# Single-row FFN gate sums, a reordered opening, and a final norm in four multiplications in a two-layer backbone kernel

## The chip, the cores and the metric

The kernel runs on one core of a Trainium2 chip, as one program. The metric is device time of one execution in microseconds (us), the median of the runs shown; lower is better. On a core, TensorE (PE) multiplies matrices, VectorE (DVE), ScalarE (ACT) and GpSimd (POOL) work on elements, and SyncE (SP) issues the DMA transfers here. Each engine executes its own instructions in order and waits on semaphores for the others.

## The reference

Two layers over 640 tokens (128 context, 512 latent) of width 1024. Each layer has a mixer (layer 0: pooling and short convolution; layer 1: grouped-query attention) and a SwiGLU FFN, each behind an RMSNorm with a shift, a scale and a gate that come from a conditioning vector; one last RMSNorm ends it.

```python
def ada_params(cvec, w_ada, b_ada):
    m = jax.nn.silu(cvec) @ w_ada + b_ada
    return jnp.split(m[:, None, :], 6, axis=-1)

for l in range(DEPTH):
    sh1, sc1, g1, sh2, sc2, g2 = ada_params(cond, w_ada[l], b_ada[l])
    h = rms_norm(x, norm_g[l, 0]) * (1 + sc1) + sh1
    x = x + g1 * mixer(h)
    h = rms_norm(x, norm_g[l, 1]) * (1 + sc2) + sh2
    x = x + g2 * ((silu(a) * b) @ w_out)      # a, b = split(h @ w_in)
y = rms_norm(x, final_g)
```

Context tokens take a learned condition, latent tokens a given one, so every adaLN parameter is a pair of values. Outputs are the two parts of y and the new keys and values.

## The kernel before, in words

**Layout.** The residual stream lies in the on-chip memory as `x[128, 8, 640]`: eight blocks of 128 features, tokens along the row. All float32 products are split: an operand is kept as a high and a low half (`ah`/`al`, `wh`/`wl`), and a product is three matmul passes (high by high, low by high, high by low). One output block of 128 features by 640 tokens from 1024 input features takes 8 x 3 x 2 matmuls of 128x320.

**Weights.** `Weights` streams them from memory in order (`raw_...`, issued by SP), three raw buffers ahead; ACT rounds the high half (`wh`, L144) and DVE subtracts for the low half (`wl`, L145). PE, the only user, takes them in the order of the program.

**Stages of layer 0.** The opening computes two of the six adaLN chunks (2 is the first half of the mixer's scale, 3 the second) on PE (`ada_pe` L298, `ada_row` L322, `ada_turn` L327), scales x with them (`prep` L478: ACT writes `ah`, DVE writes `al`), multiplies the first three blocks of the mixer's input weights (`first_mm` L795) and sums the squares of x for the norm (`Norm.add` L430: the first four blocks square and add on POOL, the last four square on ACT and add on POOL). Then `project("pi")` does 13 more input blocks beside the pooling and convolution (`mixer_in` L999), and `project("po")` the eight output blocks. The FFN has three groups of 8, 8 and 6 hidden blocks: the first group begins with 4 plain blocks (8 products), all other hidden blocks are "fast" ones (`fast_blocks` L619): a unit of seven quarter-size products (numbered 1 to 7) instead of eight, each of 12 matmuls in the trace, with weight sums made on DVE (lines L236 to L242) and products combined by DVE into `uv` (L652). After each group `project("fo0_...")` multiplies eight output blocks, and `residual`/`update` (L515, L501) adds each block, times the gate, to x: three DVE instructions (L506). A PSUM tile holds an output block until it has been evacuated, so PE must wait for a late DVE or ACT when it comes round to the tile. In layer 1 the mixer is attention; its FFN is the same, with a last projection `last1` (L1432) that ends in the final norm.

**Rows of adaLN.** All other adaLN values are sums on DVE: `AdaDve.run(n)` (L357) does n rows. One row is 128 of the 6 x 1024 values of a layer, from one transfer of 512 KB (`rawa`, L354): four reductions of 128x512 over `rawa` times `silb` (L371, each with a small read of its accumulator). A list of jobs `(layer, first row, number of rows)` sets their order; when a job's last row is summed, `ada_done` (L389) makes the values usable, and a set `known` holds what may be used. At the end of a row the next transfer is issued.

**Where rows are run.** The call sites set how many rows are summed beside each block: the opening, the callback `each` of `project("pi")` (`1 + (i < 7) - (i >= 11)` for block i, 18 rows), the plain blocks of the FFN (3 rows), the fast units (the callback `fast_each`, at product 6 of a unit: every unit of group 0, every second unit of groups 1 and 2), and `project("fo0_...")` (`1 + i % 2`, 12 rows in each). In layer 1, `gates` runs the eight rows of the FFN's gate in group 0, two rows in each of its four units. `EARLY = 30` is the number of rows loaded before layer 0's FFN.

**Final norm.** `last1` treats tokens in two spans (384 and 256). `nrm.finish` makes `rstd` of a span with a matmul, three ACT and three DVE instructions; `out(cols, step)` (L1443) then multiplies block by block (two of three blocks on DVE, one on POOL, L1446) and issues an output transfer for every two blocks (L1449).

## Time and profile before

| | before |
|---|---|
| runs (3): median, lowest, highest | 1377.84 us, 1377.27, 1378.74 |
| the profiled execution: time / span | 1376.99 us / 1375.2 us |
| mean granted TensorE clock | 0.986 |
| PE busy / DVE busy | 1327.7 us (97%) / 1081.2 us (79%) |
| ACT busy / POOL busy | 636.3 us (46%) / 70.3 us (5%) |
| moved by DMA | 155.54 MB, mean 113 GB/s |
| the chain that ended last, by engine | PE 77%, DVE 16%, ACT 3%, issue 2%, DMA 1% |

The span reaches from the first to the last instruction that the profiler records; the execution's own time is 1.8 us longer. The granted clock is a share of TensorE's 2.4 GHz: 1.0 and 0.5 (1.2 GHz) are its two levels. A busy PE does useful work at either level, so a stretch can be full and still be slow. The clock and the idle time of PE are thus read together: where PE waits, and what PE gets done per microsecond in a stage against a like stage elsewhere.

### The profile page before, as it was taken

The page shows a single profiled execution, that of the slowest core. Times are in us where ns is not written, and L with a number is a line of the kernel's source. Part 1 is how long each engine was busy: PE and PEld are TensorE (multiplying, and loading weights), DVE is VectorE, ACT ScalarE, POOL GpSimd, SP SyncE. Part 2 cuts the span into 40 slices and gives each one's busy share as a digit, 9 for nine tenths or more (in the row PEclk, how much of TensorE's full clock was granted, in tenths as well). Part 3 has the DMA queues.
Part 4 walks back from the last instruction along what each step waited for, and adds up shares of the span by engine and source line. Part 5 has one row for each costly group of instructions (what it writes and reads, how often), then busy time and mean ns, then how long its engine had stood idle before and what let it go on. Part 6 is the DMA issues. An engine that isn't in the chain of part 4 may idle for free.

```text
span 1375.2 us, 22538 instructions
## 1 busy us (share of the span) xinstructions
PE 1327.7 (97%) x8929; PEld 1294.1 (94%) x8929; DVE 1081.2 (79%) x2182; ACT 636.3 (46%) x1155; POOL 70.3 (5%) x73
## 2 busy tenths in 40 slices
PE   6989999989999999999999999999999999999995
PEld 3889999989999999999998899999999999999995
DVE  4899988999988898789976777689993577446745
ACT  3532335744135531454565675477551255314543
POOL 3200000000000000000013121000000000000013
PEclk7999999999999999999999999999999999999998
DMA  9635523134533254324531110031242122311212
GB/s 363 250 117 176 195 93 123 64 106 169 172 123 114 95 187 154 108 92 140 188 95 55 43 49 34 32 134 53 106 154 77 62 76 78 123 62 62 77 47 77
DMA packets 36872, 155.54 MB, mean 113 GB/s; under 512 B 4000, under 2 KB 11168, under 8 KB 26016
## 3 DMA queue, kind: packets, MB, share of 16 engines
q1 hardware_dynamic: 36768, 154.12, 32.2%
q8 instruction: 70, 1.15, 0.3%
q14 instruction: 34, 0.28, 0.1%
HBM read 148.60 MB, written 2.88 MB: 110 GB/s over the span
## 4 chain that ended last, share of the span: by engine, by line
PE 77%; DVE 16%; ACT 3%; issue 2%; DMA 1%; SPq 0%; POOL 0%; DVEq 0%; ACTq 0%; POOLq 0%
PE fi L630 24%; PE fo L289 21%; PE fi L289 7%; PE pq L289 5%; PE pi L289 5%; DVE junk L371 5%; PE po L289 4%; DVE wl_fi_p L145 3%; PE wb L289 2%; PE wa L289 2%; PE o L1326 2%; PE s L1276 1%; PE t L1309 1%; ACT wh_fi_p L144 1%; DMA raw_ada<-wada 1%
## 5 line engine op out<-in xcount | busy, mean ns | idle before, releaser
L144 ACT ACTIVATE wh_fi_p<-raw_fi 128x512 fp32r<-128x512 f32 x252 | 153.9, 626 | 219.5 <-PE fi L630 108.6
L371 DVE CUSTOM_DVE_ANT_0 junk<-rawa,silb 128x512 f32<-128x512 f32 x336 | 237.0, 705 | 6.5 <-DMA rawa<-wada 2.2
L145 DVE TENSOR_TENSOR wl_fi_p<-raw_fi,wh_fi_p 128x512 fp32r<-128x512 f32 x252 | 170.1, 686 | 64.1 <-ACT wh_fi_p L144 63.9
L506 DVE SCALAR_TENSOR_TENSOR x<-fo,mod,x 128x128 f32<-128x128 f32 (+1 forms) x144 | 55.5, 433 | 94.1 <-PE fo L289 90.8
L144 ACT ACTIVATE wh_fo<-raw_fo 128x1024 fp32r<-128x1024 f32 (+1 forms) x48 | 47.5, 990 | 145.4 <-PE fo L289 121.2
L630 PE MATMUL fi<-bh,wh_fi_p 128*128 128x320 f32 x288 | 89.0, 309 | 0.7 <-DVE x L506 0.5
L630 PE MATMUL fi<-bh,wl_fi_p 128*128 128x320 f32 x288 | 88.9, 309 | 0.6 <-DVE wl_fi_p L145 0.6
L630 PE MATMUL fi<-ah,wl_fi_p 128*128 128x320 f32 x288 | 88.8, 308 | 0.0
L630 PE MATMUL fi<-al,wh_fi_p 128*128 128x320 f32 x288 | 88.7, 308 | 0.0
L630 PE MATMUL fi<-ah,wh_fi_p 128*128 128x320 f32 x288 | 88.4, 307 | 0.0
L630 PE MATMUL fi<-bl,wh_fi_p 128*128 128x320 f32 x288 | 88.4, 307 | 0.0
L289 PE MATMUL fo<-al,wh_fo 128*128 128x320 f32 x352 | 80.8, 310 | 0.0
L289 PE MATMUL fo<-ah,wh_fo 128*128 128x320 f32 x352 | 80.6, 310 | 0.1
L289 PE MATMUL fo<-ah,wl_fo 128*128 128x320 f32 x352 | 80.4, 309 | 0.0
L289 PE MATMUL fo<-bh,wh_fo 128*128 128x320 f32 x328 | 75.2, 310 | 0.0
L289 PE MATMUL fo<-bh,wl_fo 128*128 128x320 f32 x328 | 75.0, 310 | 0.0
L289 PE MATMUL fo<-bl,wh_fo 128*128 128x320 f32 x328 | 74.9, 310 | 0.0
L630 PE MATMUL fi<-x0h,wh_fi_p 128*128 128x320 f32 x216 | 69.0, 323 | 5.0 <-DVE uv L652 3.6
L630 PE MATMUL fi<-xh,wh_fi_p 128*128 128x320 f32 x216 | 68.0, 320 | 2.6 <-DVE uv L652 2.1
L630 PE MATMUL fi<-x0l,wh_fi_p 128*128 128x320 f32 x216 | 66.9, 311 | 0.0
L630 PE MATMUL fi<-x0h,wl_fi_p 128*128 128x320 f32 x216 | 66.9, 311 | 0.0
L289 PE MATMUL pi<-ah,wh_in 128*128 128x320 f32 (+1 forms) x256 | 62.3, 326 | 4.7 <-ACT ev L526 3.8
(375 smaller groups left out, 3808.7 us busy)
## 6 DMA issues: line engine op xcount, KB each, us to landing
raw_fi<-wfi SPq DMA_DIRECT2D x44, 1024.0 KB, 4.8
rawa<-wada SPq DMA_DIRECT2D x84, 512.0 KB, 3.4
raw_fo<-wfo SPq DMA_DIRECT2D x16, 1024.0 KB, 4.9
raw_ada<-wada SPq DMA_DIRECT2D x12, 512.0 KB, 9.9
raw_in<-win SPq DMA_DIRECT2D x6, 1024.0 KB, 6.4
raw_fo<-wfo SPq DMA_DIRECT2D x8, 768.0 KB, 4.2
raw_qkv<-wqkv SPq DMA_DIRECT2D x6, 1024.0 KB, 5.0
raw_out<-wout SPq DMA_DIRECT2D x4, 1024.0 KB, 4.8
```

Of the source, the lines that this page charges most:

```text
L144: S.activation(h, src, AF.Copy)
L145: eng.tensor_tensor(out=l, in0=src, in1=h.bitcast(F32), op=ALU.subtract)
L289: PE.matmul(ps[:, h, 0 : hi - lo], w[a][:, k, cols], rhs[b][:, k0 + k, lo:hi], start=k == 0 and a == b, stop=k == kn - 1 and a == 1,)
L371: op = V.tensor_tensor_reduce(out=self.junk, in0=raw[:, cols], in1=self.silb[:, c, cols], scale=1.0, scalar=0.0, op0=ALU.mult, op1=ALU.add ...
L506: V.scalar_tensor_tensor(out=xs, in0=got[:, 0 : b - a], scalar=mod[l][:, gate0 + m, c : c + 1], in1=xs, op0=ALU.mult, op1=ALU.add,)
L630: PE.matmul(out, w[a][:, k, :], ops.get(OPERAND[p], b)[:, k, :], start=fresh and k == 0 and a == b, stop=k == ops.kn - 1 and a == 1, skip_ ...
L1276: PE.matmul(self.ps[:, hf, 0:HT], bufB[a][:, self.h, q0 : q0 + P], kt[b][:, self.kv, hf * HT : hf * HT + HT], start=n == 0, stop=n == 2,)
L1309: PE.transpose(flat(pt)[:, s * P : s * P + P], self.pe[:, s * P : s * P + P], ident)
L1326: PE.matmul(po[:, 0 : 2 * P], vt[a][:, self.kv, s * P : s * P + P], got[b][:, s, :], start=s == 0 and n == 0, stop=s == 4 and n == 2,)
```

## The change

- **Opening.** The weights of the first input blocks are loaded ahead of the four quarters of chunk 3. PE gets matmuls of zeros into a tile that is not yet used (`turn_over`: 6, 3 and 14 of 128x512). The matmuls of chunk 3 come behind the first half of the first block instead of ahead of it. The squares of x are all made by ACT (`nrm.square`), and their sums are DVE instructions (`add_square(V)`); POOL has none. The two rows that were summed together at the end of the opening's first part have four of these sums between them.
- **Rows in layer 0.** The FFN's gate (rows 40 to 47) becomes eight jobs of one row, which are summed in `fo0_0`, each ahead of the block that needs it. `EARLY` goes from 30 to 28. Rows by stage, before and after: `pi` 18 and 16 (two rows beside blocks 5 to 7 instead of 0 to 6, none left out at the end), plain blocks of the FFN 3 and 0, fast group 0 4 and 0, `fo0_0` 12 and 12, fast group 1 4 and 8, `fo0_1` 12 and 14 (1, 1, then 2 beside each block), fast group 2 3 and 6.
- **Rows in layer 1.** The FFN's gate becomes eight jobs of one row, one beside each block of `fo1_0`, with two transfers issued ahead; group 0 has none.
- **Final norm.** `out(ks, cols)` multiplies four blocks at once on DVE by `rstd` repeated along the block axis, and issues one transfer for them: four multiplications and four transfers in place of 16 and 8. The first follows the first span's `rstd`, the other three stand behind the second span's, whose `finish` has priority.

```diff
@@ -34,7 +34,7 @@
-EARLY = 30
+EARLY = 28
@@ -500,7 +500,7 @@
-        assert (l, gate0 // 8, 8) in known
+        assert any((l, gate0 // 8, n) in known for n in range(m + 1, 9))
@@ -731,13 +731,20 @@
-                project(f"fi{l}_{gi}", xin, KB, 2 * plain, in_done, ext=True, each=each and (lambda i: each(i, True)))
+                project(f"fi{l}_{gi}", xin, KB, 2 * plain, in_done, ext=True, each=each and (lambda i: each(i, gi, True)))
...
-                project(f"fo{l}_{gi}", hid, f1 - f0, KB, lambda k, ps: residual(ps, k, l, 40), each=each)
+                project(
+                    f"fo{l}_{gi}",
+                    hid,
+                    f1 - f0,
+                    KB,
+                    lambda k, ps: residual(ps, k, l, 40),
+                    each=each and (lambda i: each(i, gi)),
+                )
@@ -759,15 +766,18 @@
-            [(0, 4, 4)] + [(0, 8 * p, 8) for p in (2, 4, 3, 5)] + [(1, 8 * p, 8) for p in (1, 0, 2, 4, 3)]
+            [(0, 4, 4)]
+            + [(0, 8 * p, 8) for p in (2, 4, 3)]
+            + [(0, 40 + b, 1) for b in range(8)]
+            + [(1, 8 * p, 8) for p in (1, 0, 2, 4, 3)]
...
+        ws.load(1, cut=True)
...
-        ws.load(1, cut=True)
@@ -795,33 +805,50 @@
+        idle = first[2][:, 0, :]
+
+        def turn_over(n):
+
+            for _ in range(n):
+                PE.matmul(idle, zeror, zeror2, start=True, stop=True)
+
+        turn_over(6)
...
-        ada_pe(3, acc[3], range(1))
+        turn_over(3)
...
-        ada_pe(3, acc[3], range(1, 4))
+        turn_over(14)
...
-            nrm.add(k, pool_only=True)
-        prep(0, bufA, 0, 0)
-        prep(1, bufA, 0, 0)
-        prep(2, bufA, 0, 0)
-        ws.split(0, ahead=False)
+            prep(k, bufA, 0, 0)
+            if k == 1:
+                ws.split(0, ahead=False)
+        ws.split(1, ahead=False)
+        for k in range(4):
+            nrm.square(k)
+        first_mm(0, range(4))
+        ada_pe(3, acc[3], range(4))
...
-        prep(3, bufA, 0, 0)
-        ws.split(1, ahead=False)
-        first_mm(0, range(0, 2))
+        nrm.add_square(V)
+        nrm.add_square(V)
+        nrm.add_square(V)
+        nrm.add_square(V)
+        first_mm(1, range(2))
...
-        first_mm(0, range(2, 4))
-        first_mm(1, range(4))
+        first_mm(1, range(2, 4))
...
-            nrm.add(k)
+            nrm.square(k)
...
-        ada.run(2, hold=False)
+        ada.run(1, hold=False)
+        nrm.add_square(V)
+        nrm.add_square(V)
+        nrm.add_square(V)
+        nrm.add_square(V)
+        ada.run(1, hold=False)
@@ -1021,7 +1048,7 @@
-            each=lambda i: ada.run(1 + (i < 7) - (i >= 11)),
+            each=lambda i: ada.run(1 + (5 <= i < 8)),
@@ -1051,8 +1078,8 @@
-                each=lambda i, plain=False: ada.run(int(i >= 5) if plain else 1 + i % 2),
-                fast_each=lambda gi, n, p: ada.run(int(p == 6 and (gi == 0 or n % 2))),
+                each=lambda i, gi, plain=False: ada.run(0 if plain else 1 + (i % 2 if gi == 0 else int(i > 1))),
+                fast_each=lambda gi, n, p: ada.run(int(p == 6 and gi > 0)),
@@ -1440,13 +1467,13 @@
-        def out(cols, step):
-            for k in range(KB):
-                xs = x[:, k, cols]
-                (G if k % 3 == 1 else V).tensor_tensor(out=xs, in0=xs, in1=rstd[:, cols], op=ALU.mult)
-                if k % step == step - 1:
-                    ks = slice(k + 1 - step, k + 1)
-                    nc.sync.dma_start(yT[:, ks, cols], x[:, ks, cols])
+        def out(ks, cols):
+            n = cols.stop - cols.start
+            xs = x[:, ks, cols]
+            V.tensor_tensor(
+                out=xs, in0=xs, in1=rstd[:, None, cols].broadcast_to((P, ks.stop - ks.start, n)), op=ALU.mult
+            )
+            nc.sync.dma_start(yT[:, ks, cols], xs)
@@ -1468,26 +1495,31 @@
-            nrm.finish((lo, hi), None)
+            with tc.high_priority():
+                nrm.finish((lo, hi), None)
...
-        for h, (lo, hi) in enumerate(spans):
-            out(slice(lo, hi), 2)
+            if not h:
+                out(slice(0, 4), cols)
+        for h, ks in ((0, slice(4, 8)), (1, slice(0, 4)), (1, slice(4, 8))):
+            out(ks, slice(*spans[h]))
...
-    gates = AdaDve([(1, 40, 8)], 76)
+    gates = AdaDve([(1, 40 + b, 1) for b in range(8)], 76)
...
+    gates.load()
+    gates.load()
...
-        fast_each=lambda gi, n, p: gates.run(int(gi == 0 and p in (1, 6))),
+        each=lambda i, gi, plain=False: gates.run(0 if plain or gi else 1),
...
```

Three places show what moves. First PE in the opening, from the first matmuls on; `adap` and `adat` are the two steps of an adaLN chunk, `pi_152` and `pi_153` the first two input blocks, `pi_154` the third's tile. Before:

```order
L306 MATMUL adap_155<-raw_ada_2_101,silc 2x512 x2
L306 MATMUL adap_155<-raw_ada_3_103,silc 2x512 x2
L306 MATMUL adap_157<-raw_ada_0_107,silc 2x512 x2
L330 MATMUL adat_171<-kc,row_167 128x2 x4
L306 MATMUL adap_157<-raw_ada_1_109,silc 2x512 x2
L306 MATMUL adap_157<-raw_ada_2_111,silc 2x512 x2
L306 MATMUL adap_157<-raw_ada_3_113,silc 2x512 x2
L289 MATMUL pi_152<-ah,wh_in_0_204 128x320 x2
L289 MATMUL pi_152<-al,wh_in_0_204 128x320 x2
```

After:

```order
L306 MATMUL adap_161<-raw_ada_2_101,silc 2x512 x2
L306 MATMUL adap_161<-raw_ada_3_103,silc 2x512 x2
L813 MATMUL pi_154<-zeror 128x512 x3
L330 MATMUL adat_178<-kc,row_173 128x2 x4
L813 MATMUL pi_154<-zeror 128x512 x14
L289 MATMUL pi_152<-ah,wh_in_0_207 128x320 x2
L289 MATMUL pi_152<-al,wh_in_0_207 128x320 x2
...
L289 MATMUL pi_152<-ah,wl_in_0_208 128x320 x2
L306 MATMUL adap_163<-raw_ada_0_110,silc 2x512 x2
L306 MATMUL adap_163<-raw_ada_1_112,silc 2x512 x2
```

The four quarters of chunk 3 (`adap_157` before, `adap_163` after) move from ahead of the turning step of chunk 2 and of the first block to behind the block's first 24 matmuls.

Second DVE in `pi`, up to the multiplication that empties the next PSUM tile (`ev`, L521, the same line in both); a `junk` row and the `got` row behind it are one reduction. Before:

```order
L914 TENSOR_TENSOR s_4_588<-s_4_588,kc 128x2x8 x2
L371 ISA junk,got_16_591<-rawa_371,silb 128x512
L371 ISA got_16_591 128x1
L915 SCALAR_TENSOR_TENSOR pl_747<-s_4_588,up_578 128x128
L371 ISA junk,got_16_591<-rawa_371,silb 128x512
L371 ISA got_16_591 128x1
L915 SCALAR_TENSOR_TENSOR pl_747<-s_4_588,up_578 128x512
L371 ISA junk,got_16_591<-rawa_371,silb 128x512
L371 ISA got_16_591 128x1
L521 TENSOR_TENSOR ev_754<-pi_676,rstd 128x640
```

After:

```order
L941 TENSOR_TENSOR s_4_613<-s_4_613,kc 128x2x8 x2
L371 ISA junk,got_16_616<-rawa_396,silb 128x512
L371 ISA got_16_616 128x1
L942 SCALAR_TENSOR_TENSOR pl_760<-s_4_613,up_603 128x128
L942 SCALAR_TENSOR_TENSOR pl_760<-s_4_613,up_603 128x512
L521 TENSOR_TENSOR ev_767<-pi_695,rstd 128x640
```

From the pooling's step on `s_4` to `ev` there are three reductions before and one after; between this `ev` and the one ahead of it there are nine and six.

Third DVE at the end of `fo0_1`: the update of its last block (`fo_1_7`), behind which the first weights of fast group 2 stand (`wl_fi_16_p`). Before:

```order
L506 SCALAR_TENSOR_TENSOR x<-fo_1_7_5294,mod_77,x 128x128
L371 ISA junk,got_32_5162<-rawa_5241,silb 128x512
L371 ISA got_32_5162 128x1
L506 SCALAR_TENSOR_TENSOR x<-fo_1_7_5294,mod_77,x 128x192
L371 ISA junk,got_32_5162<-rawa_5241,silb 128x512
L371 ISA got_32_5162 128x1
L506 SCALAR_TENSOR_TENSOR x<-fo_1_7_5294,mod_77,x 128x320
L145 TENSOR_TENSOR wl_fi_16_p_5400<-raw_fi_16_4964,wh_fi_16_p_5399 128x512
L145 TENSOR_TENSOR wl_fi_16_p_5400<-raw_fi_17_5096,wh_fi_16_p_5399 128x512
```

After:

```order
L506 SCALAR_TENSOR_TENSOR x<-fo_1_7_5321,mod_77,x 128x128
L371 ISA junk,got_32_5330<-rawa_5260,silb 128x512
L371 ISA got_32_5330 128x1
L506 SCALAR_TENSOR_TENSOR x<-fo_1_7_5321,mod_77,x 128x192
L371 ISA junk,got_32_5330<-rawa_5268,silb 128x512
L371 ISA got_32_5330 128x1
L506 SCALAR_TENSOR_TENSOR x<-fo_1_7_5321,mod_77,x 128x320
L371 ISA junk,got_32_5330<-rawa_5268,silb 128x512
L371 ISA got_32_5330 128x1
L145 TENSOR_TENSOR wl_fi_16_p_5428<-raw_fi_16_4971,wh_fi_16_p_5427 128x512
L371 ISA junk,got_32_5330<-rawa_5268,silb 128x512
```

The reductions now run on past the update: one stands between its last instruction and the weights, where there was none, and more stand among the weights.

## Rows read from the trace of the kernel before

**Rows 1.** The page, busy time, share of the span and instructions of each engine.

```profile
PE 1327.7 (97%) x8929; PEld 1294.1 (94%) x8929; DVE 1081.2 (79%) x2182; ACT 636.3 (46%) x1155; POOL 70.3 (5%) x73
```

**Rows 2.** The waits of PE: waiting operation, what it waited for, total us, times, longest.

```profile
PE fi L630 <- DVE uv L652: 5.8, 3, 3.6
...
PE pi L289 <- ACT ev L526: 3.8, 1, 3.8
...
PE ms_a L464 <- DVE ssq_a L474: 1.5, 1, 1.5
```

**Rows 3.** Timeline, opening, PE: start, duration, engine, line, operation, [idle before <- releaser].

```profile
14.43 1.03 PE L306 MATMUL adap<-raw_ada,silc 128*2 128x512 f32 x4 [3.80 <-DMA raw_ada<-wada]
15.38 1.45 PE L330 MATMUL adat<-kc,row 98*128 98x2 f32 x8
```

**Rows 4.** The same, opening, ACT.

```profile
30.57 3.73 ACT L483 ACTIVATE ah<-x,sc 128x128 fp32r<-128x128 f32 x8 [7.02 <-DVE sc L401]
...
36.02 2.61 ACT L438 ACTIVATE sq_a<-x 128x640 f32<-128x640 f32 x4
```

**Rows 5.** The same, opening, DVE and POOL.

```profile
36.88 0.69 DVE L371 CUSTOM_DVE_ANT_0 junk<-rawa,silb 128x512 f32<-128x512 f32 x1
...
37.61 1.94 DVE L371 CUSTOM_DVE_ANT_0 junk<-rawa,silb 128x512 f32<-128x512 f32 x1
...
54.06 0.17 DVE L392 TENSOR_TENSOR mod<-got,sm 128x8 f32<-128x8 f32 x1
54.14 0.48 DVE L474 SCALAR_TENSOR_TENSOR ssq_a<-ms_a,ssq_a 128x320 f32<-128x320 f32 x1
...
36.89 8.03 POOL L440 TENSOR_TENSOR ssq_a<-ssq_a,sq_a 128x640 f32<-128x640 f32 x4 [13.42 <-ACT sq_a L438]
```

**Rows 6.** The same, input projection, DVE and PE.

```profile
87.55 0.81 DVE L521 TENSOR_TENSOR ev<-pi,rstd 128x640 f32<-128x640 f32 x1
...
88.69 0.90 PE L289 MATMUL pi<-ah,wh_in 128*128 128x320 f32 x2 [3.76 <-ACT ev L526]
```

**Rows 7.** Stretches: us, busy (x instructions) of PE, PEld, DVE, ACT, POOL, clock, DMA share, GB/s.

```profile
16.00:33.00 17.00, 12.64 (x47) 9.01 (x48) 12.83 (x18) 8.63 (x17) 7.15 (x5) 0.50 1.05 389
...
87.60:94.40 6.80, 5.71 (x21) 5.72 (x22) 6.80 (x20) 0.80 (x3) 0.00 (x0) 0.50 0.35 111
...
280.70:337.50 56.80, 52.33 (x339) 50.54 (x338) 53.50 (x108) 27.05 (x53) 0.00 (x0) 0.97 0.38 132
337.50:393.90 56.40, 56.40 (x385) 56.40 (x384) 52.34 (x130) 9.52 (x12) 0.00 (x0) 1.00 0.49 168
393.90:495.30 101.40, 101.17 (x678) 98.71 (x677) 85.34 (x157) 51.37 (x102) 0.00 (x0) 1.00 0.34 115
495.30:552.60 57.30, 57.21 (x386) 56.94 (x386) 52.31 (x131) 9.77 (x12) 0.00 (x0) 1.00 0.49 166
...
974.20:1027.30 53.10, 50.62 (x340) 49.21 (x339) 53.00 (x119) 26.63 (x52) 0.00 (x0) 1.00 0.38 127
1027.30:1084.00 56.70, 56.70 (x386) 56.70 (x385) 23.14 (x41) 9.73 (x12) 0.00 (x0) 1.00 0.24 87
1084.00:1184.60 100.60, 100.51 (x676) 98.15 (x675) 73.08 (x114) 52.19 (x102) 0.00 (x0) 1.00 0.25 85
```

**Rows 8.** A stretch inside fast group 0 of layer 0, with a row of reductions.

```profile
315.00:328.00 13.00, 13.00 (x89) 12.74 (x89) 12.48 (x29) 6.80 (x14) 0.00 (x0) 1.00 0.36 121
```

**Rows 9.** Timeline, start of fast group 2 of layer 0, PE.

```profile
555.02 0.39 PE L630 MATMUL fi<-bh,wh_fi_p 128*128 128x320 f32 x1 [0.48 <-DVE x L506]
...
557.95 0.41 PE L630 MATMUL fi<-x0h,wh_fi_p 128*128 128x320 f32 x1 [0.95 <-ACT fi L642]
```

**Rows 10.** Timeline, the end: DVE and SP.

```profile
1362.17 4.83 DVE L1446 TENSOR_TENSOR x<-x,rstd 128x384 f32<-128x384 f32 x5
...
1363.61 8.53 SPq L1449 DMA_DIRECT2D yT<-x  x8
...
1368.15 3.35 DVE L1446 TENSOR_TENSOR x<-x,rstd 128x256 f32<-128x256 f32 x5
```

## The prediction

> **What bounds the kernel now.** I read the page first: PE is busy 97% of the span [rows 1], so a gain is either PE idle time that goes or PE time at the half clock that goes. The waits of PE name the idle time: behind DVE's `uv`, behind `ev`, which empties a PSUM tile, behind the norm's sum [rows 2], and in the opening behind the transfer of chunk 3 [rows 3]. Then I read the stretches [rows 7]. The reader is to see two things there. First the clock: 0.50 from 16.0 to 33.0 and from 87.6 to 94.4, and 0.97 in layer 0's fast group 0. Each of the last two comes right behind a stop of PE of 3.6 to 3.8 us [rows 2, 6]; the stop of 1.5 us at the norm [rows 2] fell in a stretch that stayed at full clock. Second, like stages at unlike speed. A fast group of 8 units (56 products) takes 100.6 us in layer 1, where DVE has no reductions and is busy 73.1 of it: 1.80 us a product. Layer 0's group 0 (28 products) takes 56.8 us, 2.03 each; layer 1's group 0 takes 53.1 us, with DVE busy 53.0 of it. So in both groups 0 DVE is the bound, and elsewhere PE is.
>
> The sum is made against the profiled execution, 1376.99 us (span 1375.2); the median of the runs is 1377.84, 0.85 us above it. A difference under 0.2%, 2.8 us, can hardly be told from no change.
>
> **The price of a row.** Group 1 of layer 0 has four rows and DVE busy 85.3 us; layer 1's has none and 73.1 [rows 7]. So a row is (85.3 - 73.1) / 4 = 3.06 us of DVE, a little over four reductions of 0.69 [rows 5].
>
> **1. Opening: +6.0 us (from -2.4 to +7).** What sets its end is a chain: chunk 3 turned, scale, ACT's `ah` of blocks 4 to 7 at 30.57 [rows 4], squares, rows of reductions, weights of block 2, the norm's sum at 54.14 [rows 5], and behind it everything. Two links get shorter.
>
> The start: `adat` of chunk 2 issues at 15.38 only because chunk 3's first quarter, in front of it on PE, waits 3.80 us for its transfer [rows 3]. That goes, so the first block can begin earlier. Chunk 3 now lands behind two weight transfers of 512 KB: 1 MB at the 389 GB/s of that stretch [rows 7] is 2.7 us later. Its first quarter landed at about 14.4, and at that rate the other three 4.0 us after; with the 2.7 all is there at about 21. The first block's first 24 matmuls run ahead of it on PE: 24 x 0.147 (56.7 us for 386 [rows 7]) are 3.5 us. With `ah`, `al` and weights by about 18 to 20 and PE at full clock, they end by about 23 and chunk 3, a quarter of which takes 1.0 us [rows 3], by about 24.5; turned and scaled it lets ACT begin at 26.1, not 30.57. So the `ah` of blocks 4 to 7 comes 4.5 us earlier.
>
> The sums: POOL's four additions of 128x640 take 8.03 us, and while they run a reduction takes 1.94 us on DVE instead of 0.69; four of them do so [rows 5], 5.0 us in excess. By the Trainium skill, "SBUF — State Buffer" (section on the engine and DMA ports), DVE with two inputs and GpSimd hold a shared port pair in turn and the loser blocks for a whole instruction; by that a reduction could be held for up to a whole POOL addition, 2.0 us, and the excess would be 8.0. The row has 1.25 each, and the row decides. These sums now cost DVE four additions at the price of a 128x640 operation, 0.81 at most [rows 6]: 3.2 us (the four of blocks 0 to 3 fall into DVE's waits for chunk 3). Net 1.8. ACT's extra squares, 4 x 0.65 [rows 4], fall into its idle 7.02 us [rows 4]. Together 4.5 + 1.8 = 6.3, less a little for the order: 6.0. The low bound is rival B below. The turning-over matmuls stand ahead of nothing that is ready: 14 of 128x512, each 1.6 times one of 128x320, are 3.3 us at full clock and 6.6 at half, while weights and `al` of the first block take until about 18.
>
> **2. Input projection: +4.7 us (+1.5 to +7).** PE stops 3.76 us because the tile that it needs is emptied by `ev`, which DVE starts at 87.55 behind nine reductions since the `ev` ahead of it [rows 6]; six are left. Three less are 3 x 0.69 less some overlap, 1.85 us: the stop becomes 1.9 us. From 88.69 to 94.4 PE then worked at half clock [rows 6, 7], which costs 5.7 / 2 = 2.85 us. I take it that a stop of 1.9 us leaves the clock alone, as the one of 1.5 us did: 1.85 + 2.85 = 4.7. If the clock falls all the same, +1.85. What is late next is the next block's `ev`, with one reduction more per block than that; DVE is full up to 166, but PE has only short waits there.
>
> **3. Fast group 0 of layer 0: +5.8 us (+4 to +6.5).** 56.8 us against 28 x 1.80 = 50.3: 6.5 lost, 3.6 of it in one wait behind `uv` [rows 2], and some 1.7 at the half clock behind that wait. Three rows of the plain blocks and four of the group, 21 us of DVE, go. The group becomes like layer 1's group 1; I leave 0.7 for its first unit, where operands are still made.
>
> **4. Fast groups 1 and 2 of layer 0: 0 (0 to -7).** They get four and three rows more. Group 1: 85.3 + 4 x 3.06 = 97.6 of 101.4 us, 96% busy, so DVE still fits. The nearest row for such a load is a unit in group 0: DVE busy 12.48 of 13.0 us with a row of reductions, PE busy all 13.0 [rows 8]. I take 0, as the cover there was enough; if it is gone, a row costs up to 3.06 each.
>
> **5. Start of fast group 2: -2.6 us (0 to -5.5).** Two rows more in `fo0_1`, eight reductions of 0.69: 5.5 us of DVE in a stage that leaves it 57.3 - 52.3 = 5.0 idle [rows 7], all in the late blocks. The last update is already late: the group's first products wait 0.48 us for x and 0.95 us for ACT [rows 9]. I put the last update half of the 5.5 later, rounded. `fo0_0` has as many rows as before, and the 14 small operations that the gate's single rows add, 0.17 us each [rows 5], are 2.4 us of the 56.4 - 52.3 = 4.1 that DVE has idle there [rows 7]: 0.
>
> **6. Fast group 0 of layer 1: +2.3 us (+1.5 to +2.8).** 53.1 against 50.3; its eight rows are what fills DVE. `fo1_0`, where they go, has DVE busy 23.1 of 56.7 [rows 7]; with 24.5 more it is 47.6, and no row here bounds PE: 0.
>
> **7. End: +2.1 us (+1 to +3.2).** Five multiplications of 384 take DVE 4.83 us beside POOL's, then five of 256 take 3.35; the eight transfers are issued from 1363.61 on for 8.53 us [rows 10]. Two multiplications of 4 x 384 at the price of 640 in 0.81 [rows 6] are 2 x 1.94 at most, two of 4 x 256 are 2 x 1.30. DVE's work after `rstd` is then 6.5 us in place of 8.2, and POOL no longer stands beside it. With only the last transfers bigger, some 1.7 to 2.5 us arrive at the end.
>
> **Sum.** 6.0 + 4.7 + 5.8 + 0 - 2.6 + 2.3 + 2.1 = 18.3. 1376.99 - 18.3 = 1358.7; against the median 1377.84 - 18.3 = **1359.5 us**.
>
> **Rivals.**
> A. DVE becomes the bound in groups 1 and 2. Evidence for it: at 96% little slack is left for the order within a unit, and in layer 1's group 0 a fully busy DVE cost 2.8 us. Against: [rows 8]. If a third of the seven rows lands on PE, 7 us: 1366.5. Chance 0.14.
> B. The clock stays at half through the opening. For: it was 0.50 from 16 to 33 with PE busy 12.6 of 17.0 us [rows 7]. Then the first block's 24 matmuls take 7.0 us and end at about 26, chunk 3 is turned about 4 us later, ACT begins where it does now, and only the sums' 1.8 us or less is won; with the turning-over matmuls, 6.6 us, in the way of ready work as well, the opening loses 2.4. Against: PE now has work where it had stopped. By the Trainium skill, "TensorE: Matmul & The Clock Gate" (Part 1, the HAM clock gate), half clock is the default and sustained activity releases it, which speaks for the turning over; the same rule lets the clock drop where PE waits 2.6 us for its first weights and again for chunk 3. With +1 in place of +6.0: 1364.5. Chance 0.14.
> C. The stop in the input projection still brings half clock: 1359.5 + 2.85 = 1362.4. Chance 0.08.
> D. Slower. The nine rows more in group 1 to group 2 of layer 0 (seven in the groups, two in `fo0_1`) are not hidden at all: 9 x 3.06 = 27.5 us on PE's path. The other terms give 20.9, so the change turns slower once more than 20.9 of the 27.5 land: at the full price 1377.84 - 20.9 + 27.5 = 1384.4. Against: DVE's idle time of 16.1 us in group 1 [rows 7] would all have to be of no use. Chance 0.03.
> E. The reductions only move and the opening gains nothing, since 1 MB of weights ahead of chunk 3 takes back what POOL's absence gives, and each group waits for something else: within 0.2%. Chance 0.02.
>
> **How the numbers follow.** Forecast 0.59, A 0.14, B 0.14, C 0.08, D 0.03, E 0.02. The forecast's own cases lie from 1353 (all terms near their good ends) to 1363. A and B, with C, reach to about 1369; the range is 1353 to 1369, and leaves out both ends' corners, D and E. Faster 0.94, same 0.02, slower 0.04 (D, and A with B at their worst).
>
> **What would show it.** Right: the norm's sum at about 48, not 54; no wait over 2.5 us in the input projection and clock 1.00 there; group 0 of both layers at about 1.80 us a product; group 1 of layer 0 at 101 to 102 us with DVE at 96%; the span ends at about 1357, four transfers behind the end. Wrong: clock 0.50 from 20 to 30, a group 1 over 104 us, or waits of PE for `wl` or `uv` in groups 1 and 2.

## The result, and the profile after

The changed kernel takes 1358.85 us (median of 4 runs, 1356.08 to 1359.53) against 1377.55 us before (4 runs): a ratio of 0.9859, 95% interval 0.9842 to 0.9876, so 18.7 us or 1.4% faster. The forecast was 1359.5 in a range of 1353 to 1369. The profiled execution took 1358.93 us, its span 1356.8, 18.4 less than before.

First the page of the changed kernel: busy times, and the granted clock over 40 slices.

```profile
span 1356.8 us, 22590 instructions
PE 1326.3 (98%) x8952; PEld 1295.5 (95%) x8952; DVE 1083.6 (80%) x2211; ACT 638.5 (47%) x1159; POOL 46.3 (3%) x56
...
PEclk9899999999999999999999999999999999999998
```

PE does the same products, and 23 matmuls of zeros beside them, in 18 us less. Its busy time is nearly that of [rows 1]; what went is 17 us of its idle time (47.5 us before, 30.5 now) and some of its time at half clock (mean clock 0.986 before, 0.993 now). The waits of PE say which:

```profile
PE pi L289 <- DVE wl_in L145: 2.9, 2, 2.5
...
PE pi L289 <- ACT ev L526: 1.9, 1, 1.9
...
PE fi L630 <- DVE x L506: 1.6, 1, 1.6
...
PE fi L630 <- ACT fi L642: 0.9, 1, 0.9
PE adap L306 <- DMA raw_ada<-wada: 0.8, 3, 0.3
...
PE fi L630 <- DVE uv L652: 0.2, 1, 0.2
```

The wait behind `uv` is gone (5.8 to 0.2 us), the one behind `ev` is halved (3.8 to 1.9) [rows 2], and the one for the transfers of adaLN chunks, 3.80 us of it in [rows 3], went from 6.4 us to 0.8. The wait at the start of fast group 2, behind the last update of x, has grown from 0.48 to 1.63 [rows 9]. The stretches that answer to [rows 7] (us, then busy time and instructions of PE, PEld, DVE, ACT, POOL, granted clock, DMA share, GB/s):

```profile
12.00:36.00 24.00, 23.05 (x147) 18.56 (x150) 17.45 (x35) 16.80 (x28) 0.00 (x0) 1.00 1.05 386
40.80:47.60 6.80, 5.64 (x23) 5.64 (x24) 6.56 (x17) 0.94 (x3) 0.00 (x0) 0.50 1.01 408
81.80:85.20 3.40, 3.40 (x15) 3.40 (x14) 3.40 (x9) 0.00 (x0) 0.00 (x0) 0.50 0.02 5
...
271.55:321.70 50.15, 50.12 (x339) 49.22 (x338) 37.82 (x60) 26.26 (x51) 0.00 (x0) 1.00 0.26 86
...
378.10:479.55 101.45, 101.12 (x678) 98.64 (x677) 94.20 (x190) 51.42 (x102) 0.00 (x0) 1.00 0.40 136
479.55:536.90 57.35, 57.26 (x387) 56.99 (x387) 54.82 (x139) 9.81 (x12) 0.00 (x0) 1.00 0.52 180
536.90:615.64 78.74, 76.03 (x508) 73.81 (x507) 73.38 (x156) 37.59 (x76) 0.00 (x0) 1.00 0.38 128
959.90:1010.30 50.40, 50.37 (x339) 49.17 (x339) 37.81 (x60) 26.31 (x52) 0.00 (x0) 1.00 0.27 86
1010.30:1067.10 56.80, 56.80 (x388) 56.80 (x387) 44.88 (x117) 9.84 (x12) 0.00 (x0) 1.00 0.36 129
```

Both groups 0 now take 50.2 and 50.4 us, the speed of the groups without reductions. Group 1 of layer 0 carries eight rows in place of four, DVE is busy 94.2 of 101.45 us in place of 85.3, and PE has lost nothing. The clock is full from 12 to 36, where it was 0.50 from 16 to 33; it is 0.50 in two other places, 40.8 to 47.6 and 81.8 to 85.2.

The three ends of the opening and the tail, as [rows 4, 5, 6, 10] (timeline: start, duration, engine, line, operation, idle before and its releaser). ACT and DVE in the opening:

```profile
25.95 3.74 ACT L483 ACTIVATE ah<-x,sc 128x128 fp32r<-128x128 f32 x8 [2.54 <-DVE sc L401]
```

```profile
32.27 0.69 DVE L371 CUSTOM_DVE_ANT_0 junk<-rawa,silb 128x512 f32<-128x512 f32 x1
...
34.35 3.61 DVE L428 TENSOR_TENSOR ssq_a<-ssq_a,sq_a 128x640 f32<-128x640 f32 x4
...
47.97 0.48 DVE L474 SCALAR_TENSOR_TENSOR ssq_a<-ms_a,ssq_a 128x320 f32<-128x320 f32 x1
```

PE behind the late evacuation, and DVE and SP at the end:

```profile
81.26 0.56 PE L289 MATMUL pi<-ah,wh_in 128*128 128x320 f32 x2 [1.92 <-ACT ev L526]
```

```profile
1345.24 3.42 DVE L1473 TENSOR_TENSOR x<-x,rstd 128x1536 f32<-128x1536 f32 x2
...
1347.07 5.56 SPq L1476 DMA_DIRECT2D yT<-x  x4
...
1349.82 2.36 DVE L1473 TENSOR_TENSOR x<-x,rstd 128x1024 f32<-128x1024 f32 x2
```

Where the 18.4 us of span came from, by the times at which each stage's first PE or DVE instruction starts in the two traces:

| part | predicted | measured in the trace |
|---|---|---|
| 1. opening: the norm's sum at 54.14, now 47.97 | +6.0 | +6.2, of which 5.6 are left at the next evacuation (76.58, now 70.99) |
| 2. input projection, up to fast group 0 (280.71, now 271.55) | +4.7 | 9.2 - 5.6 = +3.6 |
| 3. fast group 0 of layer 0: 56.83, now 50.18 | +5.8 | +6.65 |
| 4. fast group 1: 101.35, now 101.44 | 0 | -0.1 |
| 5. fast group 2 with its start: 77.56, now 78.74 | -2.6 | -1.2 |
| 6. fast group 0 of layer 1: 53.03, now 50.43 | +2.3 | +2.6 |
| 7. PE's end to the span's end: 12.19, now 10.72 | +2.1 | +1.5 |
| sum | 18.3 | 18.4, with -0.2 in the stages between |

How well such times repeat can be read from the profiles below. Up to fast group 0 of layer 0 the program is the same in the changed kernel and in experiments 5, 6, 7, 8 and 10, and in these six profiles the norm's sum stands at 47.19 to 47.97 and the group starts at 268.99 to 271.61. The changed kernel's own 47.97 and 271.55 are late ones among them. So parts 1 and 2 together are 9.1 to 11.7 us against the one profile of the kernel before, and a start that differs by less than 2.6 us shows nothing by itself.

### The profile page after: what moved, and what is told of

It reads as the page before. It is cut to its first block, busy times and chain, and to the rows that moved or that the text cites. A ratio compares the mean times of both kernels' runs of the same rounds, so it can differ in the third digit from the quotient of the medians.

```text
span 1356.8 us, 22590 instructions
## 1 busy us (share of the span) xinstructions
PE 1326.3 (98%) x8952; PEld 1295.5 (95%) x8952; DVE 1083.6 (80%) x2211; ACT 638.5 (47%) x1159; POOL 46.3 (3%) x56
## 4 chain that ended last, share of the span: by engine, by line
PE 82%; DVE 11%; ACT 3%; issue 2%; DMA 2%; SPq 0%; POOL 0%; DVEq 0%; ACTq 0%; POOLq 0%
PE fi L630 28%; PE fo L289 19%; PE fi L289 8%; PE pi L289 6%; PE pq L289 5%; PE po L289 4%; DVE junk L371 3%; PE wb L289 2%; PE wa L289 2%; PE o L1353 2%; PE s L1303 2%; DVE wl_fi_p L145 1%; PE t L1336 1%; DMA rawa<-wada 1%; DMA x<-xT 1%
## 5 line engine op out<-in xcount | busy, mean ns | idle before, releaser
L371 DVE CUSTOM_DVE_ANT_0 junk<-rawa,silb 128x512 f32<-128x512 f32 x336 | 232.6, 692 | 6.0 <-DMA rawa<-wada 1.0
L144 ACT ACTIVATE wh_fo<-raw_fo 128x1024 fp32r<-128x1024 f32 (+1 forms) x48 | 47.5, 990 | 147.5 <-PE fo L289 128.8
L630 PE MATMUL fi<-xl,wh_fi_p 128*128 128x320 f32 x216 | 66.5, 309 | 0.0
L630 PE MATMUL fi<-xh,wl_fi_p 128*128 128x320 f32 x216 | 66.5, 309 | 0.0
```

Of the source, the lines that this page charges most:

```text
L144: S.activation(h, src, AF.Copy)
L371: op = V.tensor_tensor_reduce(out=self.junk, in0=raw[:, cols], in1=self.silb[:, c, cols], scale=1.0, scalar=0.0, op0=ALU.mult, op1=ALU.add ...
L630: PE.matmul(out, w[a][:, k, :], ops.get(OPERAND[p], b)[:, k, :], start=fresh and k == 0 and a == b, stop=k == ops.kn - 1 and a == 1, skip_ ...
```

## The experiments

Theory: the seven parts are separate gains, each where PE was idle or at half clock behind a late DVE, and DVE has room for a row wherever it is not already full. Rivals, part by part, stand in each expectation. Each kernel is the changed one with the edit shown. A time is compared as its ratio to the kernel before, of the runs made beside it; the changed kernel has 0.9859 (0.9842 to 0.9876). Since each of these parts is a few microseconds, what decides is read in the trace, the stop or the stretch that the edit is about and where a stage starts, within the spread just given; the ratio says only whether the whole agrees.

**1. No matmuls of zeros**

```diff
-        turn_over(6)
-        turn_over(3)
-        turn_over(14)
```

> The changed kernel without the 23 matmuls of zeros in the opening. Theory (the zeros keep the granted clock up): the clock is 0.50 for some stretch between 12 and 33 us, the first block's 24 matmuls take about 7 us in place of 4, chunk 3 is turned 2 to 4 us later than at 24.56, the norm's sum comes at 50 to 51 in place of 47.97, and the time is 2 to 5 us above the changed kernel's 1358.9. Rival (the zeros do nothing, since the order of the work alone sets the opening's end): norm's sum within 0.5 us of 47.97 and the time within 1.5 us.

Measured: 0.9868 (0.9853 to 0.9883), median 1359.57 us. The clock falls as expected, and for 6.7 us:

```profile
14.30:21.00 6.70, 4.89 (x17) 4.67 (x18) 6.53 (x10) 6.70 (x12) 0.00 (x0) 0.50 1.06 398
21.00:24.00 3.00, 3.00 (x24) 1.29 (x23) 1.69 (x3) 0.33 (x1) 0.00 (x0) 0.99 1.00 420
```

The timeline of PE and DVE in this kernel gives what it cost:

```profile
16.11 0.90 PE L289 MATMUL pi<-ah,wh_in 128*128 128x320 f32 x2 [3.36 <-ACT wh_in L144]
```

```profile
49.29 0.49 DVE L474 SCALAR_TENSOR_TENSOR ssq_a<-ms_a,ssq_a 128x320 f32<-128x320 f32 x1
```

Without the zeros PE stands still for 3.36 us, the first half of the first block then runs at half clock, and the norm's sum is 1.3 us later than 47.97, and later than in all six profiles above. Fast group 0 starts at 272.64, 1.0 us behind the latest of the six; the whole is 0.7 us longer, which the ratios can't tell from nothing. The mechanism is the theory's, the price below what was expected. In the changed kernel chunk 3's matmuls start at 20.46 and wait for their last transfer until 21.74; here they start at 22.18 with everything landed and end 1.3 us later than there. So only the last part of the slow stretch lies on the path. Rival B, to which the prediction gave 5 us, had the clock at half through the opening, and the zeros themselves in the way; this run, with 6.7 us of half clock and no zeros, prices a part of it and not the whole.

**2. The sums of squares back on POOL**

```diff
         ada.run(1, hold=False)
-        nrm.add_square(V)
-        nrm.add_square(V)
-        nrm.add_square(V)
-        nrm.add_square(V)
+        nrm.add_square(G)
+        nrm.add_square(G)
+        nrm.add_square(G)
+        nrm.add_square(G)
         ada.run(1, hold=False)
```

> The changed kernel with the last four additions of squares back on POOL, beside the reductions. Theory (a reduction beside a POOL addition is held, 1.94 us in place of 0.69): four reductions of 1.9 us, 5.0 us more, less the 3.6 us that the additions now take on DVE: the norm's sum at 49.4 in place of 47.97 and the time 1 to 2 us above the changed kernel. Rival (POOL's additions cost DVE nothing, and the gain of the opening is the order alone): reductions of 0.69, the norm's sum 3.6 us earlier and the time 2 to 4 us below.

Measured: 0.9873 (0.9856 to 0.9889), median 1359.59 us, the norm's sum at 49.05, 1.1 us later than 47.97 and later than in all six profiles. DVE's and POOL's timeline:

```profile
31.72 2.06 DVE L371 CUSTOM_DVE_ANT_0 junk<-rawa,silb 128x512 f32<-128x512 f32 x1
...
33.83 1.92 DVE L371 CUSTOM_DVE_ANT_0 junk<-rawa,silb 128x512 f32<-128x512 f32 x1
```

```profile
31.66 7.43 POOL L428 TENSOR_TENSOR ssq_a<-ssq_a,sq_a 128x640 f32<-128x640 f32 x4 [29.75 <-ACT sq_a L422]
```

Four reductions take 1.9 to 2.06 us while POOL adds, and 0.69 as soon as it has ended, as before the change [rows 5]: shown by putting the additions there and taking them away. By the Trainium skill, "SBUF — State Buffer" (the section on the engine and DMA ports), the loser of the shared port pair blocks for the whole of the other's instruction. POOL's four additions here, 1.86 us each, have their own waits for DVE in them. What POOL takes alone is seen in the kernel before, where DVE is idle until 16.87:

```profile
13.16 1.25 POOL L436 TENSOR_TENSOR ssq_a<-x 128x640 f32<-128x640 f32 x1 [11.27 <-DMA x<-xT]
...
15.71 1.53 POOL L440 TENSOR_TENSOR ssq_a<-ssq_a,sq_a 128x640 f32<-128x640 f32 x1
```

A reduction is held for 1.2 to 1.4 us, about what one such operation of 1.25 to 1.53 us takes alone, so the trace agrees with the rule as nearly as it can tell. The 2.0 us that the prediction took for a whole POOL addition had POOL's waits in it, and so had its 8.0 us.

**3. The rows of the input projection as they were**

```diff
-            each=lambda i: ada.run(1 + (5 <= i < 8)),
+            each=lambda i: ada.run(1 + (i < 7) - (i >= 11)),
```

> The changed kernel with the rows beside the input projection as they were (18 rows, two beside each of blocks 0 to 6). Theory (the late evacuation stops PE, and the stop lowers the clock): PE's stop in front of the fifth block is 3.5 to 4 us in place of 1.92, half clock for 6 to 7 us behind it in place of 3.4, and the time 3 to 4.5 us above the changed kernel. Rival (the projection gained only because the opening gives DVE a head start, its own rows do not matter): a stop of about 2 us and the time within 1 us.

`EARLY` goes back to 30 with it. Measured: 0.9890 (0.9875 to 0.9905), median 1362.71 us. The stop and the clock behind it, from PE's timeline and the stretches:

```profile
83.53 0.90 PE L289 MATMUL pi<-ah,wh_in 128*128 128x320 f32 x2 [3.77 <-ACT ev L526]
```

```profile
82.00:93.00 11.00, 9.47 (x45) 9.47 (x46) 11.00 (x31) 2.74 (x6) 0.26 (x6) 0.69 0.31 98
```

A clock of 0.69 over 11 us is 6.8 us at half. Fast group 0 starts at 275.57, 4.0 us later than 271.55 and than any of the six profiles: the 1.85 of the stop and half of some 3.4 us more at half clock, which is the theory's account, and a little more. The new opening alone does not shorten the stop: it is as long as before [rows 6], and so is the half clock [rows 7], while the group starts 5.1 us earlier than the 280.71 of the kernel before. So some 5 us are the opening's part.

**4. Rows back in layer 0's fast group 0 and its plain blocks**

```diff
-  each=lambda i, gi, plain=False: ada.run(0 if plain else ...),
-  fast_each=lambda gi, n, p: ada.run(int(p == 6 and gi > 0)),
+  each=lambda i, gi, plain=False: ada.run(int(i >= 5) if plain else ...),
+  fast_each=lambda gi, n, p: ada.run(int(p == 6)),
```

> The changed kernel with three rows again beside the plain blocks of layer 0's FFN and one in each unit of fast group 0 (later groups then run out of rows earlier). Theory (the rows in front of uv are the whole loss of that group): a wait of PE behind uv of 3 to 4 us, 28 products in 56 to 57 us in place of 50.2, some of it at half clock, and the time 5 to 7 us above, less up to 1 us that fewer rows later give back. Rival (DVE has room since the opening left it ahead): below 52 us and the time within 2 us.

Measured: 0.9913 (0.9898 to 0.9928), median 1365.88 us, 7.0 above. The group's stretch and PE's stop:

```profile
269.10:326.45 57.35, 52.64 (x340) 50.84 (x339) 54.43 (x118) 27.10 (x53) 0.00 (x0) 0.97 0.39 130
```

```profile
285.03 0.61 PE L630 MATMUL fi<-x0h,wh_fi_p 128*128 128x320 f32 x1 [3.91 <-DVE uv L652]
```

57.35 us, the stop behind `uv` and a clock of 0.97: the whole loss of the kernel before comes back with these seven rows, though the opening and the projection are the new ones.

**5. Layer 1's gate rows back in its group 0**

```diff
-  each=lambda i, gi, plain=False: gates.run(0 if plain or gi else 1),
+  fast_each=lambda gi, n, p: gates.run(int(gi == 0 and p in (1, 6))),
```

> The changed kernel with layer 1's eight gate rows back in fast group 0 (two in each unit) in place of fo1_0. Theory: DVE is the bound of that group again, 28 products in 53 us in place of 50.4, the time 2.3 to 2.8 us above the changed kernel. Rival (the group was slow for another reason, its operands or its first weights): within 0.5 us of 50.4.

Measured: 0.9894 (0.9879 to 0.9909), median 1363.42 us.

```profile
961.20:1015.20 54.00, 50.84 (x339) 49.15 (x339) 54.00 (x133) 26.73 (x52) 0.00 (x0) 1.00 0.39 124
```

DVE is busy all 54.0 us and the group is 3.6 us longer than 50.4; before the change it was 2.6 longer. DVE executes 133 instructions there in place of 119 [rows 7]: the 14 small ones of single-row jobs, the likely source of the rest, which no run takes apart. This execution also had a clock of 0.50 for 6.8 us (540.9 to 547.7) at the start of layer 0's fast group 2, which the edit does not touch and which is part of its time.

**6. The final norm as it was**

```diff
-            if not h:
-                out(slice(0, 4), cols)
-        for h, ks in ((0, slice(4, 8)), (1, slice(0, 4)), (1, slice(4, 8))):
-            out(ks, slice(*spans[h]))
+        for h, (lo, hi) in enumerate(spans):
+            out(slice(lo, hi), 2)
```

> The changed kernel with the final norm as it was (16 multiplications on DVE and POOL, eight transfers). Theory: from the last matmul of the program to the end of the span 12.2 us in place of 10.7, the time 1.5 us above. Rival (the transfers at the end set it, and they move the same bytes): within 0.4 us.

The edit takes back the whole part of the diff on `last1`, `out` and the priority too. Measured: 0.9879 (0.9862 to 0.9895), median 1360.40 us; from PE's end to the span's end 1358.2 - 1346.4 = 11.8 us in place of 10.7. PE's last two matmuls took 1.10 us there and 0.70 in the changed kernel, so the first multiplication is the better mark: it starts 13.05 us ahead of the span's end, 13.03 before the change, and 11.56 with it. The tail's part is thus 1.5 us, less than the 2.1 of the prediction. Its sum had DVE's work at 6.5 us; it is 3.42 + 2.36 = 5.8. What it had wrong is the end: the last transfers are of 512 KB and take 3.5 us from issue to landing (median), those of 256 KB before took 2.3, and behind DVE's last multiplication 4.6 us pass in place of 3.7.

**7. Two rows in every unit of fast group 1**

```diff
+  fast_each=lambda gi, n, p: ada.run(int(p == 6 and gi > 0) * (2 if gi == 1 else 1)),
```

> The changed kernel with two rows in each unit of layer 0's fast group 1 (16 in place of 8; the rows then end with fast group 2, and the last projection of layer 0 has none). It asks where DVE's cover ends. Theory (a row is 3.06 us of DVE and is free until DVE is full): the group has 101.4 us and DVE about 95 of them; eight rows more are 24.5 us, of which about 6 fit: the group takes 118 to 121 us and DVE is busy throughout, the time 15 to 20 us above. Rival (no row is free, each costs PE its full price): the group 24 to 26 us longer. Second rival (DVE has room that its busy time does not show): less than 8 us.

Measured: 0.9934 (0.9919 to 0.9949), median 1368.41 us, 9.6 above. The group and the two stages behind it:

```profile
377.20:486.45 109.25, 103.25 (x680) 99.00 (x678) 108.79 (x253) 53.42 (x102) 0.00 (x0) 1.00 0.47 159
486.45:543.90 57.45, 56.40 (x384) 56.40 (x384) 55.04 (x140) 9.91 (x12) 0.00 (x0) 1.00 0.55 186
543.90:625.20 81.30, 77.43 (x508) 75.20 (x507) 73.14 (x153) 37.53 (x76) 0.00 (x0) 0.98 0.35 114
```

DVE is full (108.8 of 109.25), so this is past the turning point, but the group is only 7.8 us longer, where 17 to 20 were expected and 24 without any cover. The second rival holds. Some 7 us of the added work went into DVE's idle time. The stages behind are 2.6 us longer, but not because work of DVE slid into them, which is as busy there as in the changed kernel (55.0 and 73.1 us, there 54.8 and 73.4): PE's stop at the start of group 2 is 2.79 us in place of 1.63, and the clock is 0.98 there in place of 1.00.

And a row is cheaper than the prediction had it: from four rows to eight the group's DVE time rose by 94.2 - 85.3 = 8.9 us [rows 7], 2.2 each and not 3.06. The prediction took the difference of two layers' groups for the price of four rows, sixteen reductions. In the stretch of [rows 7] DVE did 21, five more at its two ends, of rows that belong to the stages around it; 12.3 us over 21 reductions are 0.58 each and 2.3 a row.

**8. The rows of fo0_1 early**

```diff
-  ... 1 + (i % 2 if gi == 0 else int(i > 1))
+  ... 1 + (i % 2 if gi == 0 else int(i < 6))
```

> The changed kernel with fo0_1's 14 rows placed early: two beside each of blocks 0 to 5 and one beside 6 and 7, in place of one, one and then two. Theory (the rows beside the last blocks make the last update late): the first fast unit of group 2 goes without its stops of 1.63 and 0.95 us and the time is 1 to 2.5 us below the changed kernel. Rival (DVE is full in the stage as a whole, so the order in it does not matter): the same stops, within 0.5 us.

Measured: 0.9886 (0.9871 to 0.9900), median 1361.70 us. Not better, and the median is 2.9 us above; the theory falls. DVE's waits in the stage, and PE's first stop behind it:

```profile
DVE junk L371 <- DMA rawa<-wada: 2.2, 3, 0.8
```

```profile
539.32 0.39 PE L630 MATMUL fi<-bh,wh_fi_p 128*128 128x320 f32 x1 [3.19 <-DVE x L506]
```

The changed kernel waits 0.3 us for rows' transfers in that stage; here it is 2.2, and the stop is 3.19 us in place of 1.63. Its DVE has 2.5 us idle in 57.3 as it is. Behind the stop the clock was 0.50 for 6.8 us, where the changed kernel kept 1.00. So it is not the blocks that carry the rows that make the update late, and packed closer the rows run into their transfers; their number is what experiment 10 changes.

**9. The rows of the input projection later**

```diff
-            each=lambda i: ada.run(1 + (5 <= i < 8)),
+            each=lambda i: ada.run(int(i > 1) + (5 <= i < 10)),
```

> The changed kernel with no row beside the first two blocks of the input projection, and two beside blocks 5 to 9 (16 in all, as there). Theory (the six reductions between two evacuations are PE's remaining stop of 1.92 us there, and the half clock behind it where it falls): no stop over 0.5 us before the fifth block, granted clock 1.00 from 48 us on, fast group 0 of layer 0 starts 2 to 3.6 us earlier than at 271.55, and the time is 1.5 to 3.5 us below the changed kernel's. Rival (DVE is full through the whole projection, so the late work only comes later): stops of PE of 1 us or more appear behind 90 us, and the group starts within 1 us of 271.55.

Measured: 0.9871 (0.9856 to 0.9885), median 1360.26 us. The stop at 79 us is gone, and the clock with it is whole (76 to 90 us), but PE stops at the start of the FFN, where it did not:

```profile
76.00:90.00 14.00, 13.98 (x94) 13.71 (x93) 13.68 (x28) 7.33 (x12) 0.33 (x6) 1.00 0.32 114
```

```profile
211.64 0.75 PE L289 MATMUL fi<-ah,wh_fi 128*128 128x320 f32 x2 [1.03 <-DVE x L506]
...
214.59 0.41 PE L289 MATMUL fi<-al,wh_fi 128*128 128x322 f32 x1 [1.47 <-DVE al L499]
```

Fast group 0 starts at 271.34 against 271.55. Experiment 5, which has the stop of 1.92 us and full clock behind it, starts that group at 270.43. The rival holds: DVE is full through this stretch (70.3 of the 71.6 us from 94.4 to 166), so what is spared early is paid 130 us later.

**10. Three rows in group 0, three fewer in fo0_1**

```diff
-  ... 1 + (i % 2 if gi == 0 else int(i > 1))
-  fast_each=lambda gi, n, p: ada.run(int(p == 6 and gi > 0)),
+  ... 1 + (i % 2 if gi == 0 else int(i in (2, 4, 6)))
+  fast_each=lambda gi, n, p: ada.run(int(p == 6 and (gi > 0 or n > 0))),
```

> The changed kernel with three rows in the units 1 to 3 of layer 0's fast group 0 (none in unit 0 and in the plain blocks) and 11 in place of 14 in fo0_1 (two beside blocks 2, 4 and 6, one beside the others). Theory (DVE is full in fo0_1 and has 12 us idle in group 0, and only rows in front of the first uv hurt there): group 0 stays at 50.2 us, the stops at the start of group 2 (1.63 and 0.95 us) fall to below 1 us together, group 2 takes 76.5 to 77.5 us in place of 78.74, and the time is 1 to 2 us below the changed kernel's. Rival (any row in group 0 costs it its price, as in the kernel before): group 0 takes 53 to 57 us and the time is above.

Measured: 0.9844 (0.9830 to 0.9859), median 1356.93 us.

```profile
271.60:321.90 50.30, 50.22 (x339) 49.23 (x338) 45.20 (x90) 26.05 (x52) 0.00 (x0) 1.00 0.35 117
479.60:536.90 57.30, 57.20 (x386) 56.93 (x386) 50.19 (x127) 9.76 (x12) 0.00 (x0) 1.00 0.48 164
536.90:613.90 77.00, 75.92 (x507) 73.84 (x506) 70.00 (x144) 37.54 (x76) 0.00 (x0) 1.00 0.36 122
```

Group 0 with three rows takes 50.3 us. Experiment 4 had these three and four more, which DVE summed ahead of the group's first `uv` at 284.40, and took 57.35: rows are free here as long as none stands ahead of that first result. With 50.2 of 57.3 us of DVE in `fo0_1`, the stop behind x is gone and group 2 takes 77.0 in place of 78.74. With experiment 8 this settles part 5.

**11. A fourth chunk on PE in place of four rows in the opening**

```diff
-            [(0, 4, 4)]
-            + [(0, 8 * p, 8) for p in (2, 4, 3)]
+            [(0, 8 * p, 8) for p in (2, 4, 3)]
...
+        acc = ada_acc(0)
+        ada_pe(0, acc, range(4))
+        row = ada_row(0, acc)
         first_mm(1, range(4, 8))
-        ada.run(1, hold=False)
...
-        ada.run(1, hold=False)
         ws.split(2, ahead=False)
-        ada.run(2, hold=False)
...
+        acc = ada_acc(1)
+        ada_pe(1, acc, range(4))
+        row1 = ada_row(1, acc)
```

> The changed kernel with the four rows of the opening (rows 4 to 7 of layer 0) computed on PE as a fourth chunk, from the same number of bytes, in place of 16 reductions on DVE (11.7 us) that stand in front of the norm's sum; chunk 0 goes ahead of the second half of the second block. Theory (DVE's reductions set the opening's end: PE waits 2.50 us for the third block's weights behind them, then runs at half clock until 47): the norm's sum comes at about 40 in place of 47.97, no half clock from 41 to 47, the input projection's third block ends about 5 us earlier, its later stop of 1.92 us goes, as DVE is ahead, and the time is 5 to 9 us below the changed kernel's. Rival (PE or the transfers set it as well: the third block's weights land at 37.4 and the fourth chunk only behind them): less than 3 us below.

Measured: 0.9848 (0.9831 to 0.9864), median 1357.15 us; the norm's sum at 40.26.

```profile
36.00:55.00 19.00, 18.48 (x138) 14.32 (x138) 6.82 (x16) 6.89 (x14) 0.35 (x6) 1.00 0.86 345
76.00:90.00 14.00, 12.08 (x82) 11.81 (x81) 14.00 (x35) 6.32 (x10) 0.33 (x6) 1.00 0.41 135
```

The sum comes 7.7 us earlier, DVE is busy 6.8 of these 19 us, and PE has neither a stop nor half clock there. But nothing is left of it at fast group 0, which starts at 269.87, inside the 268.99 to 271.61 of the six profiles with the changed kernel's opening; behind the same stop of 1.92 us this execution kept its full clock. The second half of the norm stood on PE at 49.2, behind the third block's products, so the evacuations began at 52.9, as in the changed kernel (53.1). The rival holds in effect, for that reason: the head start ended at the next fixed place in the order.

**12. These three together, and an earlier second half of the norm**

```diff
         nrm.finish((0, HT), None)
+        nrm.finish((HT, T), None)
...
+        fev = [scaled_main(first[m], f"ev_{m}") for m in range(2)]
...
-        nrm.finish((HT, T), None)
...
-        row = first_bias(0)
+        rows = [first_bias(m) for m in (0, 1)]
...
```

> What the other runs point to, in one kernel: chunk 1 on PE in the opening, three rows in group 0's units 1 to 3 and 11 in fo0_1, and, so that the head start reaches the input projection, the second half of the norm directly behind the first, with the bias columns of the first two blocks turned before the third block is done. Theory (the stop of 1.92 us in the projection is DVE's backlog, which starts when the first three blocks are evacuated and biased; chunk 1 on PE alone left that point at 57 us): the first reductions of the projection start 3 us or more earlier than at 68.4, the stop is below 1 us, no half clock before the end, group 0 starts at 266 to 268, and the time is 1351 to 1354 us. Rival (the gains do not add, as the stop is set by the work between two evacuations and not by a backlog): the stop stays at 1.9 us and the time is 1355 us or more.

Here three means experiments 10 and 11 and this edit, which also puts the evacuation of the first two blocks directly behind the norm. Measured: 0.9827 (0.9813 to 0.9840), median 1353.86 us, 5 runs from 1353.72 to 1354.30. It is faster than both kernels: 24.2 us below its before, and below the changed kernel's interval. PE's stop in the projection:

```profile
80.34 0.56 PE L289 MATMUL pi<-ah,wh_in 128*128 128x320 f32 x2 [1.64 <-ACT ev L526]
```

The time is what was expected; the way is only half so. The first reductions come at 67.44, 0.9 us earlier and not 3, and the six profiles have them at 67.32 to 68.75; the stop is 1.64 and not below 1, and group 0 starts at 269.12, inside their range too. The pooling waits for the bias columns by way of ACT until 57.5. So the stop stays DVE's work between two evacuations, as the rival has it. What is left to give the time is the full clock, with which the changed kernel's fastest run took 1356.08 (mean clock 0.995), and the 1.7 us by which experiment 10 shortens group 2; that these two add up to it was not run by itself.

## Why the prediction was right

The total is right to 0.7 us, and each part that was given a size has the predicted sign. Some of the closeness is compensation: parts 1 and 2 together (9.2 for 10.7) and part 7 gave 2.1 us less than predicted, parts 3, 5 and 6 gave 2.6 more, and part 4 and the stages between lost 0.3. And the profile is one execution: in another the same opening and projection end up to 2.6 us earlier (the six profiles above), and one of the four runs took 1356.08. To within 0.7 us is luck; to within some 3 us is the sum's merit.

*Opening.* Right at both of its ends: `ah` of blocks 4 to 7 was forecast for 26.1 and starts at 25.95; the norm's sum for 48 and is at 47.97. In between two errors cancel. The first block's 24 matmuls end at 20.5 and not at 23, and chunk 3 at 22.8 and not at 24.5; but 12 matmuls of the second block, which the sum left out, stand on PE ahead of the step that turns it:

```profile
20.46 2.30 PE L306 MATMUL adap<-raw_ada,silc 128*2 128x512 f32 x16
...
24.56 0.95 PE L330 MATMUL adat<-kc,row 98*128 98x2 f32 x8
```

Experiment 2 shows the sums' share: 1.1 us against the forecast 1.8; the four additions take 3.61 us and not 3.2. Experiment 3 has the opening's gain at some 5 us where it reaches fast group 0. Rival B's half clock did not come in the place that it named; experiment 1 shows 1.3 us as the price of a part of it. What was not foreseen is a half clock from 40.8 to 47.6, which sets in during the second of two stops of 1.04 and 2.50 us, where the kernel before had full clock (36 to 48), while DVE's reductions still set the pace. Experiment 11 takes it away and gains nothing by that at fast group 0.

*Input projection.* The stop went from 3.76 to 1.92, as forecast. The step that failed is "I take it that a stop of 1.9 us leaves the clock alone": in the profiled execution the clock is 0.50 for 3.4 us behind it, 1.7 us lost. That is rival C at 1.7 of its 2.85 us, and it comes in some executions and not in others: see below.

*Group 0 of layer 0.* Right, and 0.85 us under-sized: the 0.7 held back for its first unit was not needed. Experiment 4 brings the loss back with the seven rows alone, and experiment 10 leaves it to the four of them that stand ahead of the first `uv`. *Group 0 of layer 1*: 2.6 for 2.3, experiment 5 the same way round.

*Groups 1 and 2.* Right that they cost nothing. DVE was forecast at 97.6 us busy in group 1 and is at 94.2, since a row costs 2.2 and not 3.06: the prediction divided the work of 21 reductions by four rows (experiment 7). The idle time that is left there, 7.3 us, holds three rows more at that price, so the turning point is near eleven rows (an estimate from these rows); experiment 7, with sixteen, shows that rival D's full price is not reached even past it: eight more rows cost 7.8 us in the group, not 24.

*Start of group 2.* Right in cause, and the size 1.2 for 2.6. The stop is 1.63 + 0.95 us in place of 0.48 + 0.95 [rows 9]; the first of the two is 1.21 to 2.02 in experiments 1, 2, 5, 6 and 9, which leave this place as it is. The prediction said "all in the late blocks" as if their place mattered; by experiments 8 and 10 it is DVE's whole load in the stage.

*End.* Right in kind, 1.5 for 2.1; DVE's work was put 0.7 us too high, and the larger last transfers were in the sum with too small a price (experiment 6).

## What to carry to other kernels

Where an engine other than the bound carries movable work, read for each stage how full that engine is and which of its results the bound takes first; work costs nothing in a stage with idle time unless it stands ahead of that first result (three rows free in group 0; with four more ahead of the first `uv`, 7 us lost). A stage that is already full does not get better by another order within it, and what is taken out of its front comes back at its end, 130 us later in experiment 9; here only moving the work to a stage with room paid. A gain at one place of a hand-written order lasts only to the next fixed place: look where the head start ends before counting it (7.7 us at the norm's sum in experiment 11, none at the FFN). And before a difference at one place is put down to an edit, look how far that place moves between executions of the same code (2.6 us here).
